# Around the Strassen up projection of a decoder layer: transposes moved behind two quads, difference blocks made in the stage before, the down projection's first inputs loaded in the last quads

## Chip, cores and metric

The kernel runs on one core of one Trainium2 chip. The metric is the device time in microseconds (us). TensorE multiplies (PE in the profile, PEld its weight loads), VectorE is DVE, ScalarE is ACT, GpSimd is POOL, SyncE is SP. SP's queue issues the loads from HBM, ACT's queue the stores.

## What is computed

One step of a decoder layer for 1024 prompt tokens and 8 x 4 sample tokens, model width 1024, all in float32:

```python
h = RMSNorm(x); z = h @ w_in            # u, v: chunked gMLP gating; q, k, v: windowed attention
...
merged = jnp.concatenate([rms_norm(a_out, g_out_chunk), rms_norm(b_out, g_out_attn)], axis=-1)
o = jnp.einsum('bsc,cd->bsd', merged, w_o)
x = x + rms_norm(o, g_post_mix)
h = rms_norm(x, g_pre_ffn)
f = jnp.einsum('bsf,fd->bsd', jnp.square(jax.nn.relu(jnp.einsum('bsd,df->bsf', h, w_up))), w_down)
return x + rms_norm(f, g_post_ffn)
```

The change touches the stretch from w_o to the first products with w_down; w_up is 1024 x 4096, w_down 4096 x 1024.

## The kernel before

Every product is made of three fp32r products: each operand is split into a rounded part (hi) and the rest (lo), by `split`, a cast on ACT (L127) and a subtraction on DVE (L128); the terms are hi x hi, hi x lo, lo x hi. The code is in program order on every engine queue where the text below speaks of it.

**The w_o stage.** The tokens are nine tiles: the 32 sample tokens (called NCH, first) and eight tiles of 128. `proj_o` multiplies a tile by w_o in two PSUM banks; the transposes of the next tile's merged inputs (`merge_transpose`, tiles mg, two buffers) and of the previous tile's hn stand inside this stream of matmuls. `post` (L832) then makes, tile by tile: the squares of both banks (ACT, L837), ms (DVE) and r (POOL, L137 and L143), x2 = o * r * g + x (L843, L844), its squares (L851), and hn (L854), which is the input of the up projection. x2 is stored to HBM. `h_store` (L857) transposes hn with eight transposes (L67) and splits it into hT hi and lo, in two column groups: group 0 with tiles 0 to 3 and the sample tokens, group 1 with tiles 4 to 7. The four sub-blocks of Strassen's method are the two halves of the input width (k 0 to 3 and 4 to 7) by the two halves of a group's columns.

`h_sums` (L813) makes the three difference blocks sg (hi and lo) that Strassen's products 6, 7 and 3 need, and replaces one block of hT by a sum. It first adds hi and lo again on POOL (L822), and it is called for tiles 2 and 3 and the sample tokens within the stage (group 0), and for group 1 after the first part of the first quad.

**The up projection.** A quad is one pair of weight blocks (16 pairs) by one column group (2): 7 products of 12 matmuls, in `first` (products 1 and 2), `second` (6, 5, 7) and `third` (4, 3). The banks A, C, B are PSUM; product 6 and those after it add into bank A, so a copy `s` of it (L938, ACT, `snap`) has to be made between them. The parts of neighbouring quads alternate: first of quad i, third of quad i-1, second of quad i. `up_weights` loads two 512 KB blocks of w_up per pair (SP) and forms seven weight units from them (subtractions L802, L803, L806, L808 on DVE, and a split of each); the first pair's blocks are loaded into the pool `stage` (tiles raw, three buffers) before the last tile's `post`, later ones into `rawp` (tiles rw, four buffers). The results are squared (`emit`) and stored to HBM as f_d.

The order in the first quads is (0,0), (1,0), (0,1), (1,1), that is pair and group. The last tile's `h_store` and pair 1's weights come after the first part of quad (0,0).

**The down projection.** In eight rounds of four f tiles, f_d is loaded back (`f_tile`, L1004) and split, w_down likewise (`pair`, L779), and `down_one` multiplies them. All of the first round's inputs are loaded after the last quad.

## Time and profile before

| | us |
|---|---|
| time, median of 3 runs | 1129.66 (1129.57 to 1130.35) |
| the profiled execution's own time | 1130.52 |
| its span | 1128.8, mean granted TensorE clock 0.982 |
| PE busy | 1073.3 (95%) |
| DVE busy | 687.9 (61%) |
| ACT busy | 429.7 (38%) |
| POOL busy | 77.6 (7%) |
| w_o stage, up projection, down projection (start of the first matmul) | 248, 373.9, 738.3 |

PE is the bound of the kernel in the long run, and its busy share says little of the single stages. Rows of the timeline give the start, the duration of the whole group of like instructions, the engine, the line, the operation, the tiles, the count, and in brackets the idle time of the engine before it with what ended it.

### The profile page before, as it was taken

To read this page: it belongs to the slowest core of one execution; us is meant where nothing else is said; L and a number is where in the kernel's file an instruction comes from. 1 tells how busy PE (TensorE), PEld (TensorE's weight loads), DVE (VectorE), ACT (ScalarE), POOL (GpSimd) and SP (SyncE) were. 2 spreads that over 40 slices of the span, in tenths; PEclk is the share of its full clock that TensorE was granted. 3 is DMA by queue.
4 is the path that set the end of the run, shared out by engine and by line. 5 is a ranking of instruction groups with operands and counts; after the bars stand their busy time and mean duration, and the time that the engine had idled before them with its cause. 6 is when DMAs were issued, how large, how long until landed. Compare 5 with 4: busy or idle time off the path is not lost.

```text
span 1128.8 us, 17897 instructions
## 1 busy us (share of the span) xinstructions
PE 1073.3 (95%) x7053; PEld 1004.8 (89%) x7053; DVE 687.9 (61%) x1335; ACT 429.7 (38%) x934; POOL 77.6 (7%) x97
## 2 busy tenths in 40 slices
PE   7999999999989689999999999689999999999996
PEld 5888777887867689999999999689999999999996
DVE  5777877776666877656655563364544635446256
ACT  6587966564443433333323322241221312203012
POOL 2100003110142300000000000000000000000001
PEclk9999999999999889999999999989999999999998
DMA  8332201235423324233323312372431514316025
GB/s 275 136 104 75 94 24 50 94 127 179 132 93 112 112 96 125 88 111 115 102 88 115 114 50 68 104 220 59 140 98 55 152 30 122 117 36 226 9 65 187
DMA packets 52228, 121.35 MB, mean 108 GB/s; under 512 B 6945, under 2 KB 16641, under 8 KB 52129
## 3 DMA queue, kind: packets, MB, share of 16 engines
q1 hardware_dynamic: 33312, 89.44, 25.8%
q10 hardware_dynamic: 18832, 30.78, 7.3%
q8 instruction: 55, 0.90, 0.3%
q14 instruction: 29, 0.23, 0.1%
HBM read 89.43 MB, written 31.82 MB: 107 GB/s over the span
## 4 chain that ended last, share of the span: by engine, by line
PE 82%; DVE 8%; ACT 4%; POOL 2%; issue 2%; DMA 2%; SPq 0%; DVEq 0%; ACTq 0%; POOLq 0%
PE z L64 70%; PE t L64 10%; PE t L67 3%; ACT sc L527 2%; DVE w L128 1%; POOL raw L822 1%; ACT w L130 1%; DVE hT_lo L128 1%; DVE w L1048 1%; DVE pT L128 0%; POOL ro L143 0%; DVE w L1061 0%; DMA raw<-in_w_v_dram 0%; DVE w L131 0%; DMA raw<-in_w_qkv_dram 0%
## 5 line engine op out<-in xcount | busy, mean ns | idle before, releaser
L64 PE MATMUL z<-f,w 128*128 128x400 f32 (+1 forms) x2304 | 374.2, 324 | 13.5 <-ACT w L127 13.5
L64 PEld LDWEIGHTS z<-f,w 128*128 128x128 f32 x2304 | 371.8, 189 | 14.3 <-ACT w L127 13.7
L64 PE MATMUL z<-w,hT_hi 128*128 128x512 f32 (+1 forms) x768 | 210.8, 381 | 0.4 <-DVE raw L191 0.4
L1019 DVE TENSOR_TENSOR acc<-z,acc 128x400 f32<-128x400 f32 (+1 forms) x168 | 86.5, 521 | 129.8 <-PE z L64 129.6
L64 PEld LDWEIGHTS z<-w,hT_hi 128*128 128x128 f32 x768 | 134.3, 189 | 25.2 <-DVE raw L191 0.8
L64 PE MATMUL z<-hT_hi,w 128*128 128x272 f32 (+1 forms) x768 | 146.8, 286 | 0.5 <-ACT s L938 0.5
L64 PE MATMUL z<-w,hT_lo 128*128 128x512 f32 (+1 forms) x384 | 124.5, 378 | 0.0
L64 PEld LDWEIGHTS z<-hT_hi,w 128*128 128x128 f32 x768 | 122.0, 189 | 0.7 <-ACT s L938 0.7
L127 ACT CAST f<-raw 128x544 fp32r<-128x544 f32 x64 | 38.7, 633 | 202.2 <-PE z L64 152.8
L64 PE MATMUL z<-hT_lo,w 128*128 128x272 f32 (+1 forms) x384 | 109.3, 285 | 0.0
L64 PE MATMUL z<-sg,w 128*128 128x272 f32 (+1 forms) x768 | 107.5, 290 | 0.0
L64 PEld LDWEIGHTS z<-sg,w 128*128 128x128 f32 x768 | 101.2, 195 | 0.0
L938 ACT COPY s<-z 128x272 f32<-128x272 f32 (+1 forms) x96 | 36.4, 380 | 144.3 <-PE z L64 141.6
L64 PEld LDWEIGHTS z<-w,hT_lo 128*128 128x128 f32 x384 | 67.6, 188 | 14.0
L64 PEld LDWEIGHTS z<-hT_lo,w 128*128 128x128 f32 x384 | 72.9, 190 | 0.0
L128 DVE TENSOR_TENSOR w<-w 128x512 fp32r<-128x512 f32 x64 | 44.6, 703 | 34.1 <-ACT w L127 32.8
L143 POOL TENSOR_TENSOR ro<-ms,neghalf 128x1 f32<-128x1 f32 (+1 forms) x18 | 11.9, 661 | 744.5 <-DVE ms L142 744.4
L128 DVE TENSOR_TENSOR f<-raw,f 128x544 fp32r<-128x544 f32 x64 | 44.0, 706 | 27.9 <-ACT f L127 27.8
L128 DVE TENSOR_TENSOR w<-raw,w 128x512 fp32r<-128x512 f32 x69 | 45.8, 703 | 20.6 <-ACT w L127 20.4
L64 PE MATMUL t<-sg,w 128*128 128x272 f32 (+1 forms) x384 | 54.1, 291 | 3.9 <-DVE fo L956 3.9
L64 PEld LDWEIGHTS t<-sg,w 128*128 128x128 f32 x384 | 50.7, 194 | 4.1 <-DVE fo L956 4.1
L967 DVE SCALAR_TENSOR_TENSOR fo<-fo 128x544 f32<-128x544 f32 (+1 forms) x64 | 45.3, 708 | 13.2 <-ACT fo L960 10.5
(208 smaller groups left out, 1337.2 us busy)
## 6 DMA issues: line engine op xcount, KB each, us to landing
raw<-in_w_down_dram SPq DMA_DIRECT2D x32, 512.0 KB, 4.3
rw<-in_w_up_dram SPq DMA_DIRECT2D x30, 512.0 KB, 3.7
f_d<-fo ACTq DMA_DIRECT2D x32, 272.0 KB, 3.1
raw<-f_d SPq DMA_DIRECT2D x32, 272.0 KB, 2.7
f_d<-fo ACTq DMA_DIRECT2D x32, 256.0 KB, 2.6
raw<-f_d SPq DMA_DIRECT2D x32, 256.0 KB, 2.7
xT<-in_xT_prompt_dram SPq DMA_DIRECT2D x8, 512.0 KB, 5.7
raw<-in_x_prompt_dram SPq DMA_DIRECT2D x8, 512.0 KB, 4.7
```

The source lines that it names most:

```text
L64: tc.keep_in_program_order(pe.matmul(out, lhsT, rhs, start=start, stop=stop, skip_group_check=resumed))
L67: tc.keep_in_program_order(pe.transpose(out, in_, ident[:n, :n]))
L127: pin(act.copy(hi, src))
L128: pin(vec.tensor_tensor(lo, src, hi.bitcast(F32), ALU.subtract))
L130: act.activation(hi, src, AF.Copy, scale=scale)
L143: pool.tensor_tensor(out, ms[:r, 0:1], neghalf[:r, 0:1], ALU.pow)
L527: act.activation(scs[kv][:, j, 0:nk], scs[kv][:, j, 0:nk], AF.Exp, scale=-1.0, bias=nm[:, h:h + 1], accum_out=lsum[:, h:h + 1])
L822: pool.tensor_tensor(r, hi[:, ks[k], c].bitcast(F32), lo[:, ks[k], c].bitcast(F32), ALU.add)
L938: act.copy(s, self.A)
L967: vec.scalar_tensor_tensor(f, f, 0.0, f, ALU.max, ALU.mult)
L1019: vec.tensor_tensor(o, ps[:, :n], o, ALU.add)
L1048: vec.tensor_tensor(self.y[:r, hs], tp[:r], g_fin[:r, hs], ALU.mult)
```

## The change

1. **w_o stage.** `h_sums` goes; `diffs` makes the same blocks straight from the transposes in PSUM, for tiles 2, 3 and the sample tokens, and for tile 6 inside the stage too. The block of the first half of columns (tiles t - 2) is added up again by `whole`, on DVE. There is one hn buffer (pool `hnp`) instead of two, x2 is kept in the tile xr, junk has one buffer, mg one instead of two (the sample's mg is a tile raw).
2. **First quads.** The weights of pairs 0 and 1 are both loaded into raw buffers, before the quads. The last tile's `h_store` comes ahead of quad 2, which is (0,1), instead of inside quad 0. `rawp` has two buffers instead of four. The memory for the copies s (pool `snap`), for f and for rw is that of the tiles hn and xr of the stage before.
3. **Last quads.** Their order is (14,0), (15,0), (14,1), (15,1) instead of pair by pair. In the second last one, behind group 0's last product, the memory of hT0 and sg0 is given to f tiles, and the first four f tiles and the first pair of w_down blocks are loaded and split. The other w_down blocks of round 0 come after the last quad.

```diff
-        mgp = pcm.enter_context(tc.tile_pool(name="mgp", bufs=2))
+        mgp = pcm.enter_context(tc.tile_pool(name="mgp", bufs=1))
...
-        mg = merge_load(NCH, mgp, "mg")
+        mg = merge_load(NCH, stage, "raw")
...
     pph = ExitStack()
     with ExitStack() as pcx:
         sg = [None, None]
+        sgp1 = pph.enter_context(tc.tile_pool(name="sgp1", bufs=1))
         psg0 = ExitStack()
         sgp0 = psg0.enter_context(tc.tile_pool(name="sgp0", bufs=1, side="right"))
-        sg[0] = [sgp0.tile([P, 3, 4, SUB[0]], F32R, name="sg0_%d" % i) for i in range(2)]
+        sg = [[p.tile([P, 3, 4, n], F32R, name="sg%d_%d" % (g, i)) for i in range(2)]
+              for g, (p, n) in enumerate(zip((sgp0, sgp1), SUB))]
+        hnp = pcx.enter_context(tc.tile_pool(name="hnp", bufs=1))
         mp = pcx.enter_context(tc.tile_pool(name="mp", bufs=2))
+        jp = pcx.enter_context(tc.tile_pool(name="jp", bufs=1))
         gcp = pcx.enter_context(tc.tile_pool(name="gcp", bufs=1))
         g_post = gcp.tile([P, D], F32, name="g_post")
...
-        def h_sums(g, x, n):
+        def diffs(g, x, n, r11, r12, r21, a22, s1, s2):
             hi, lo = hT[g]
             sh, sl = sg[g]
             ca, cb = slice(x, x + n), slice(SUB[g] + x, SUB[g] + x + n)
...
+            vec.tensor_tensor(s1, a22, r21, ALU.add)
+            vec.tensor_tensor(s2, s1, r11, ALU.subtract)
             split(sh[:, 0, :, ca], sl[:, 0, :, ca], s2)
-            split(hi[:, 0:4, cb], lo[:, 0:4, cb], r22)
-            vec.tensor_tensor(r21, r11, r21, ALU.subtract)
-            split(sh[:, 1, :, ca], sl[:, 1, :, ca], r21)
+            split(hi[:, 0:4, cb], lo[:, 0:4, cb], s1)
+            vec.tensor_tensor(r11, r11, r21, ALU.subtract)
+            split(sh[:, 1, :, ca], sl[:, 1, :, ca], r11)
             vec.tensor_tensor(r12, r12, s2, ALU.subtract)
             split(sh[:, 2, :, ca], sl[:, 2, :, ca], r12)
+        def h_transpose(hn, h, n):
+            tp = tbank()
+            for k in range(4):
+                transpose(tp[:, k * n:(k + 1) * n], hn[:n, (4 * h + k) * P:(4 * h + k + 1) * P], n)
+            return tp[:, 0:4 * n].rearrange("p (k c) -> p k c", k=4)
+        def halves():
+            t = stage.tile([P, D], F32, name="raw")
+            return [t[:, i * 512:(i + 1) * 512].rearrange("p (k c) -> p k c", k=4) for i in range(2)]
+        def whole(t):
+            hi, lo = hcols(t)
+            rs = halves()
+            for h, r in enumerate(rs):
+                vec.tensor_tensor(r, hi[:, 4 * h:4 * h + 4].bitcast(F32), lo[:, 4 * h:4 * h + 4].bitcast(F32), ALU.add)
+            return rs
+        def h_store(t, hn, firsts=None):
+            if t == NCH:
+                hi, lo = hT[0]
+                ca, cb = slice(2 * P, 2 * P + NSH), slice(SUB[0] + 2 * P, SUB[0] + 2 * P + NSH)
+                rs = [hnp.tile([P, 4, NSH], F32, name="rs", bufs=5) for _ in range(5)]
+                for h in range(2):
+                    tp = h_transpose(hn, h, NS)
+                    split(hi[:, 4 * h:4 * h + 4, ca], lo[:, 4 * h:4 * h + 4, ca], tp[:, :, 0:NSH])
+                    act.copy(rs[h], tp[:, :, 0:NSH])
+                    if h == 0:
+                        act.copy(rs[2], tp[:, :, NSH:NS])
+                split(hi[:, 4:8, cb], lo[:, 4:8, cb], tp[:, :, NSH:NS])
+                diffs(0, 2 * P, NSH, rs[0], rs[1], rs[2], tp[:, :, NSH:NS], rs[3], rs[4])
+            elif t % 4 < 2:
+                transpose_split(*hcols(t), hn, P)
+            else:
+                hi, lo = hcols(t)
+                g, c = gcol(t)
+                r11, r12 = firsts or whole(t - 2)
+                r21, s1 = halves()
+                s2 = halves()[0]
+                act.copy(r21, h_transpose(hn, 0, P))
+                tp = h_transpose(hn, 1, P)
+                split(hi[:, 4:8], lo[:, 4:8], tp)
+                diffs(g, c.start - SUB[g], P, r11, r12, r21, tp, s1, s2)
         def post(t, zo, xr):
             r = rows(t)
             ssq2 = small.tile([P, 2], F32, name="ssqo")
             for h in range(2):
-                junk = mp.tile([P, 512], BF16, name="junk", bufs=2)
+                junk = jp.tile([P, 512], BF16, name="junk")
                 act.activation(junk[:r], zo[h][:r], AF.Square, scale=D ** -0.5, accum_out=ssq2[:r, h:h + 1])
             ro = small.tile([P, 1], F32, name="ro")
             rms_scale2(ro[:r], ssq2[:r])
-            x2 = mp.tile([P, D], F32, name="x2")
+            hn = hnp.tile([P, D], F32, name="hn")
             for h in range(2):
                 hs = slice(h * 512, (h + 1) * 512)
-                vec.scalar_tensor_tensor(x2[:r, hs], zo[h][:r], ro[:r], g_post[:r, hs], ALU.mult, ALU.mult)
-            vec.tensor_tensor(x2[:r], x2[:r], xr[:r], ALU.add)
-            store(x2_d[drow(t), :], x2[:r])
-            if t == order[-1]:
-                hn = unit().bitcast(F32).rearrange("p a b -> p (a b)")
-            else:
-                hn = mp.tile([P, D], F32, name="hn")
+                vec.scalar_tensor_tensor(hn[:r, hs], zo[h][:r], ro[:r], g_post[:r, hs], ALU.mult, ALU.mult)
+            vec.tensor_tensor(xr[:r], hn[:r], xr[:r], ALU.add)
+            store(x2_d[drow(t), :], xr[:r])
             sx = small.tile([P, 1], F32, name="sx")
-            act.activation(hn[:r], x2[:r], AF.Square, accum_out=sx[:r])
+            act.activation(hn[:r], xr[:r], AF.Square, accum_out=sx[:r])
             r2 = small.tile([P, 1], F32, name="r2")
             rms_scale(r2[:r], sx[:r], D, EPS)
-            vec.scalar_tensor_tensor(hn[:r], x2[:r], r2[:r], g_ffn[:r], ALU.mult, ALU.mult)
+            vec.scalar_tensor_tensor(hn[:r], xr[:r], r2[:r], g_ffn[:r], ALU.mult, ALU.mult)
             return hn
...
             if t == order[-1]:
                 wup0 = up_weights(0, [stage.tile([P, D], F32, name="raw") for _ in range(2)])
+                firsts = whole(order[-3])
             hns.append((t, post(t, [fold(t, z) for z in zo], xr)))
         hn = hns[0][1]
         flush()
-    pcm.close()
+    rawp = pph.enter_context(tc.tile_pool(name="rawp", bufs=2, reuse_waits="tile"))
     sp_ = pph.enter_context(tc.tile_pool(name="snap", bufs=4, reuse_waits="tile"))
     fop = pph.enter_context(tc.tile_pool(name="fop", bufs=4, reuse_waits="tile"))
-    sgp1 = pph.enter_context(tc.tile_pool(name="sgp1", bufs=1, reuse_waits="tile"))
-    rawp = pph.enter_context(tc.tile_pool(name="rawp", bufs=4, reuse_waits="tile"))
-    sg[1] = [sgp1.tile([P, 3, 4, SUB[1]], F32R, name="sg1_%d" % i) for i in range(2)]
     def up_raws():
         return [rawp.tile([P, D], F32, name="rw") for _ in range(2)]
     class Quad:
-        def __init__(self, p, g, ws):
-            self.p, self.g, self.ws = p, g, ws
-            self.n = SUB[g]
-            self.A, self.C, self.B = [b[:, 0:self.n] for b in (zbank(), zbank(), tbank())]
+        def __init__(self, p, g):
+            self.p, self.g, self.n = p, g, SUB[g]
...
-        def first(self):
+        def first(self, ws):
             n = self.n
+            self.ws = ws
+            self.A, self.C, self.B = [b[:, 0:n] for b in (zbank(), zbank(), tbank())]
             self.fa = fop.tile([P, 2, SUB[0]], F32, name="fo")[:, :, 0:n]
             self.fb = fop.tile([P, 2, SUB[0]], F32, name="fo")[:, :, 0:n]
             self.product(1, self.A, True, True)
...
+    pq = ExitStack()
+    f_pools = []
+    def f_tile(ft):
+        f = f_pools[0 if ft % 9 < 7 else 1].tile([P, 2, T], F32R, name="f")
+        for g in range(2):
+            c = slice(GBASE[g], GBASE[g] + GW[g])
+            raw = raw_load(f_d[ft][:, c], [P, GW[g]])
+            split(f[:, 0, c], f[:, 1, c], raw)
+        return f
+    ws_up = {0: wup0, 1: up_weights(1, [stage.tile([P, D], F32, name="raw") for _ in range(2)])}
+    last = NPAIR - 2
+    seq = [(0, 0), (1, 0), (0, 1), (1, 1)] + [(p, g) for p in range(2, last) for g in range(2)]
+    seq += [(last, 0), (last + 1, 0), (last, 1), (last + 1, 1)]
+    quads = [Quad(p, g) for p, g in seq]
+    for i, q in enumerate(quads):
+        if i == 2:
+            h_store(order[-1], hn, firsts)
+        q.first(ws_up[q.p])
+        if i:
+            prev = quads[i - 1]
             prev.third()
             flush()
             if prev.g == 1:
                 del ws_up[prev.p]
                 if prev.p + 2 < NPAIR:
                     ws_up[prev.p + 2] = up_weights(prev.p + 2, up_raws())
+            if i == len(quads) - 2:
+                psg0.close()
+                phg0.close()
+                f_pools.append(pq.enter_context(tc.tile_pool(name="fp", bufs=7, side="right", reuse_waits="tile")))
+                fs0 = [f_tile(ft) for ft in range(FB)]
+                ws0 = pair(a["w_down"][0, 0])
         q.second()
-        prev = q
-        if (p, g) == (NPAIR - 1, 1):
-            q.third()
-            flush()
+    q.third()
+    flush()
     pph.close()
-    psg0.close()
-    phg0.close()
+    pcm.close()
     with ExitStack() as pf:
-        fp = pf.enter_context(tc.tile_pool(name="fp", bufs=FB + 4, side="right", reuse_waits="tile"))
+        pf.enter_context(pq)
+        f_pools.append(pf.enter_context(tc.tile_pool(name="fp2", bufs=2, reuse_waits="tile")))
         accp = pf.enter_context(tc.tile_pool(name="accp", bufs=1, reuse_waits="tile"))
         rp = pf.enter_context(tc.tile_pool(name="rp", bufs=2, reuse_waits="tile"))
         acc = accp.tile([P, KT, T], F32, name="acc")
...
+        def round_weights(b, dps):
+            return [w for dp in dps for w in pair(a["w_down"][b, dp])]
+        fs, ws = fs0, ws0 + round_weights(0, range(1, KT // 2))
         for b in range(NFB):
             last = b + 1 == NFB
             if not last:
-                nxt = round_inputs(b + 1)
+                nxt = ([f_tile((b + 1) * FB + i) for i in range(FB)], round_weights(b + 1, range(KT // 2)))
...
```

On VectorE at the end of the w_o stage, before, from the last tile but one's ms on (w_4063 and w_4066 are the lower halves of the first two weight units of pair 0, raw_4059 and raw_4060 the loaded blocks):

```order
L142 SCALAR_TENSOR_TENSOR ms_3977<-ssqo_3971 128x1
L843 SCALAR_TENSOR_TENSOR x2_3980<-z_3892,ro_3976,g_post_3172 128x512
L843 SCALAR_TENSOR_TENSOR x2_3980<-z_3893,ro_3976,g_post_3172 128x512
L128 TENSOR_TENSOR w_4063<-raw_4059,w_4063 128x512
L844 TENSOR_TENSOR x2_3980<-x2_3980,xr_3890 128x1024
L128 TENSOR_TENSOR w_4066<-raw_4059,w_4066 128x512
L802 TENSOR_TENSOR w_4069<-raw_4060,raw_4059 128x512
L806 TENSOR_TENSOR w_4069<-raw_4060 128x512
L136 TENSOR_SCALAR ms_3988<-sx_3985 128x1
L803 TENSOR_TENSOR w_4070<-raw_4060,w_4069 128x512
L854 SCALAR_TENSOR_TENSOR hn_3984<-x2_3980,r2_3987,g_ffn_3173 128x1024
```

The same place after (tile 7's post begins with ms_4111; raw_4035, raw_4038 and raw_4039 are inputs of tile 6's diffs; raw_4071 is pair 0's first loaded block):

```order
L142 SCALAR_TENSOR_TENSOR ms_4111<-ssqo_4105 128x1
L825 TENSOR_TENSOR raw_4035<-raw_4035,raw_4038 128x512
L128 TENSOR_TENSOR hT1_lo_91<-raw_4038,hT1_hi_90 128x4x128
L128 TENSOR_TENSOR sg1_1_3170<-raw_4039,sg1_0_3169 128x4x128
L128 TENSOR_TENSOR sg1_1_3170<-raw_4035,sg1_0_3169 128x4x128
L827 TENSOR_TENSOR raw_4035<-raw_4035,raw_4039 128x512
L884 SCALAR_TENSOR_TENSOR hn_4114<-z_3990,ro_4110,g_post_3183 128x512
L884 SCALAR_TENSOR_TENSOR hn_4114<-z_3991,ro_4110,g_post_3183 128x512
L128 TENSOR_TENSOR sg1_1_3170<-raw_4035,sg1_0_3169 128x4x128
L885 TENSOR_TENSOR xr_3988<-hn_4114,xr_3988 128x1024
L128 TENSOR_TENSOR w_4075<-raw_4071,w_4075 128x512
L128 TENSOR_TENSOR w_4078<-raw_4071,w_4078 128x512
```

The weight units of pair 0 have moved from inside tile 6's post behind the first half of tile 7's, and the diffs of tile 6 stand in their place; hn of tile 7 is hn_4114.

On VectorE a little later, after (xr_3988 holds x2 of tile 7, raw_4102 is the sum of tile 5, w_4081 and w_4082 hold differences of weights, fo_4173 is the first output of the first quad):

```order
L844 TENSOR_TENSOR raw_4102<-hT1_hi_90,hT1_lo_91 128x512
L812 TENSOR_TENSOR w_4082<-raw_4071,w_4082 128x512
L128 TENSOR_TENSOR w_4085<-w_4082,w_4085 128x512
L128 TENSOR_TENSOR w_4088<-w_4081,w_4088 128x512
L128 TENSOR_TENSOR w_4092<-w_4081,w_4092 128x512
L128 TENSOR_TENSOR w_4096<-w_4082,w_4096 128x512
L128 TENSOR_TENSOR w_4099<-raw_4072,w_4099 128x512
L844 TENSOR_TENSOR raw_4102<-hT1_hi_90,hT1_lo_91 128x512
L136 TENSOR_SCALAR ms_4121<-sx_4118 128x1
L891 SCALAR_TENSOR_TENSOR hn_4114<-xr_3988,r2_4120,g_ffn_3184 128x1024
L966 TENSOR_TENSOR fo_4173<-z_4171,s_4187 128x272
```

The hn of tile 7 stands behind all weight units of pair 0.

On ScalarE at the first quad, before (s_4147 is the first copy of bank A):

```order
L127 CAST w_4084<-w_4070 128x512
L127 CAST w_4087<-raw_4060 128x512
L837 ACTIVATE junk_4091,ssqo_4090<-z_3994 128x512
L837 ACTIVATE junk_4093,ssqo_4090<-z_3995 128x512
L938 COPY s_4147<-z_4130 128x272
L127 CAST hT1_hi_90<-raw_4208 128x4x128
L851 ACTIVATE w_4103,sx_4104<-x2_4099 128x1024
L60 DMA x2_d_97<-x2_4099 128x1024
L127 CAST hT1_hi_90<-t_4162 128x4x128
```

and after (s_4187 is that copy; z_4170 the bank A of quad 0):

```order
L127 CAST w_4075<-raw_4071 128x512
L127 CAST w_4078<-raw_4071 128x512
L888 ACTIVATE hn_4114,sx_4118<-xr_3988 128x1024
L60 DMA x2_d_97<-xr_3988 128x1024
L127 CAST w_4085<-w_4082 128x512
L127 CAST w_4088<-w_4081 128x512
L127 CAST w_4092<-w_4081 128x512
L127 CAST w_4096<-w_4082 128x512
L127 CAST w_4099<-raw_4072 128x512
L954 COPY s_4187<-z_4170 128x272
L127 CAST w_4143<-raw_4139 128x512
```

The copy has moved behind the squares of tile 7 and seven casts of pair 0's weights, and pair 1's first cast (w_4143) stands behind the copy.

On ScalarE in the last two quads, after (f_7767, f_7776 and f_7785 are f tiles, w_7796 and w_7799 the first w_down units, z_7843 the bank A of the last quad; the row ahead of these is its first copy):

```order
L127 CAST f_7767<-raw_7772 128x512
L127 CAST f_7776<-raw_7777 128x544
L127 CAST f_7776<-raw_7781 128x512
L978 ACTIVATE fo_7694<-z_7691 128x256
L60 DMA f_d28_126<-fo_7694 128x2x256
L127 CAST f_7785<-raw_7786 128x544
L127 CAST f_7785<-raw_7790 128x512
L60 DMA f_d29_127<-fo_7695 128x2x256
L954 COPY s_7917<-z_7843 128x256
L127 CAST w_7796<-raw_7794 128x512
L127 CAST w_7799<-raw_7794 128x512
L954 COPY s_7943<-z_7843 128x256
```

Before, no cast stands between the last quad's copies; the first f cast stands behind the last store to f_d. Now the casts of f and of the first w_down pair stand between them.

## Rows read from the trace of the kernel before

**Rows 1.** Waits of TensorE: line, releaser, us in total, times, longest us.

```profile
PE z L64 <- ACT w L127: 13.5, 1, 13.5
```

**Rows 2.** Timeline of TensorE, w_o stage: start us, us, engine, line, operation.

```profile
282.27 0.68 PE L67 MATMUL t<-ident,hn 32*128 32x32 f32 x8
...
287.12 1.03 PE L67 MATMUL t<-ident,hn 128*128 128x128 f32 x8
...
330.90 1.94 PE L67 MATMUL t<-ident,hn 128*128 128x128 f32 x8 [5.12 <-DVE hn L854]
332.49 1.85 PE L64 MATMUL z<-w,hT_hi 128*128 128x512 f32 x4
...
347.01 1.06 PE L67 MATMUL t<-ident,hn 128*128 128x128 f32 x8 [1.79 <-DVE hn L854]
347.83 1.17 PE L64 MATMUL z<-w,hT_hi 128*128 128x512 f32 x4
```

**Rows 3.** Timeline of VectorE, tile 1, and of GpSimd, tile 3, w_o stage.

```profile
304.51 1.41 DVE L843 SCALAR_TENSOR_TENSOR x<-z,ro,g_post 128x512 f32<-128x512 f32 x2 [0.73 <-POOL ro L143]
...
309.27 1.28 DVE L854 SCALAR_TENSOR_TENSOR hn<-x,r,g_ffn 128x1024 f32<-128x1024 f32 x1 [0.73 <-POOL r L137]
...
325.32 3.61 POOL L822 TENSOR_TENSOR raw<-hT_hi,hT_lo 128x512 f32<-128x512 f32 x2 [2.34 <-DVE sg L128]
328.89 0.55 POOL L137 TENSOR_TENSOR r<-ms,neghalf 128x1 f32<-128x1 f32 x1
```

**Rows 4.** Timeline of TensorE, from w_o to the third quad.

```profile
373.46 0.63 PE L64 MATMUL z<-w,hT_lo 128*128 128x512 f32 x2
...
386.55 1.94 PE L67 MATMUL t<-ident,w 128*128 128x128 f32 x8 [9.45 <-DVE w L854]
...
388.14 3.07 PE L64 MATMUL z<-sg,w 128*128 128x272 f32 x12
...
403.01 3.09 PE L64 MATMUL t<-sg,w 128*128 128x272 f32 x12 [3.85 <-DVE fo L956]
...
411.86 0.28 PE L64 MATMUL z<-hT_hi,w 128*128 128x256 f32 x1
```

**Rows 5.** Timeline of ScalarE and VectorE, first quads.

```profile
374.98 0.59 ACT L837 ACTIVATE junk<-z 128x512 bf16<-128x512 f32 x1
...
376.03 0.20 ACT L837 ACTIVATION_READ_ACCUMULATOR junk<-z 128x1 f32 x1
...
398.92 2.48 DVE L128 TENSOR_TENSOR w<-w 128x512 fp32r<-128x512 f32 x4
```

**Rows 6.** Busy time by windows, then timeline of VectorE, steady quads.

```profile
core 0: us, PE busy (x) PEld busy (x) DVE busy (x) ACT busy (x) POOL busy (x), PEclk, DMA share, GB/s
460.00:700.00 240.00, 240.00 (x1956) 240.00 (x1956) 140.00 (x236) 77.68 (x168) 0.00 (x0) 1.00 0.31 97
...
464.84 0.69 DVE L802 TENSOR_TENSOR w<-rw 128x512 f32<-128x512 f32 x1 [0.57 <-PE z L64]
...
477.46 0.69 DVE L128 TENSOR_TENSOR w<-rw,w 128x512 fp32r<-128x512 f32 x1 [0.34 <-ACT w L127]
```

**Rows 7.** TensorE at the down projection, its windows; costliest group of f casts.

```profile
723.19 1.60 PE L64 MATMUL t<-sg,w 128*128 128x256 f32 x12
...
738.32 6.86 PE L64 MATMUL z<-f,w 128*128 128x400 f32 x23 [13.53 <-ACT w L127]
...
739.00:741.00 2.00, 2.00 (x8) 1.93 (x7) 1.18 (x2) 1.14 (x2) 0.00 (x0) 0.50 0.72 209
...
743.00:744.00 1.00, 1.00 (x6) 0.99 (x5) 1.00 (x2) 0.31 (x1) 0.00 (x0) 0.72 0.78 276
...
L127 ACT CAST f<-raw 128x544 fp32r<-128x544 f32 x64 | 38.7, 633 | 202.2 <-PE z L64 152.8
```

**Rows 8.** DMA issues: tiles, queue, count, KB each, median us to landing.

```profile
raw<-in_w_down_dram SPq DMA_DIRECT2D x32, 512.0 KB, 4.3
...
rw<-in_w_up_dram SPq DMA_DIRECT2D x30, 512.0 KB, 3.7
...
raw<-in_w_up_dram SPq DMA_DIRECT2D x2, 512.0 KB, 6.1
```

More of the change, by code (lines that the diff above doesn't have):

```diff
@@ L816, in h_sums @@
             ca, cb = slice(x, x + n), slice(SUB[g] + x, SUB[g] + x + n)
-            ks = (slice(0, 4), slice(4, 8))
-            ts = [stage.tile([P, D], F32, name="raw") for _ in range(3)]
-            ts = [t[:, i * 512:i * 512 + 4 * n].rearrange("p (k c) -> p k c", k=4) for t in ts for i in range(2)]
-            r11, r12, r21, r22, s2 = ts[:5]
-            for r, k, c in ((r11, 0, ca), (r21, 0, cb), (r22, 1, cb), (r12, 1, ca)):
-                pool.tensor_tensor(r, hi[:, ks[k], c].bitcast(F32), lo[:, ks[k], c].bitcast(F32), ALU.add)
@@ L823, in h_sums @@
-            vec.tensor_tensor(r22, r21, r22, ALU.add)
-            vec.tensor_tensor(s2, r22, r11, ALU.subtract)
+            vec.tensor_tensor(s1, a22, r21, ALU.add)
+            vec.tensor_tensor(s2, s1, r11, ALU.subtract)
             split(sh[:, 0, :, ca], sl[:, 0, :, ca], s2)
-            split(hi[:, 0:4, cb], lo[:, 0:4, cb], r22)
-            vec.tensor_tensor(r21, r11, r21, ALU.subtract)
-            split(sh[:, 1, :, ca], sl[:, 1, :, ca], r21)
+            split(hi[:, 0:4, cb], lo[:, 0:4, cb], s1)
@@ L969, in emit @@
             store(f_d[2 * self.p + i][:, c0:c0 + 2 * self.n].rearrange("p (s c) -> p s c", s=2), f)
-    ws_up = {0: wup0}
-    seq = [(0, 0), (1, 0), (0, 1), (1, 1)] + [(p, g) for p in range(2, NPAIR) for g in range(2)]
-    prev = None
-    for i, (p, g) in enumerate(seq):
-        q = Quad(p, g, ws_up[p])
-        q.first()
-        if i == 0:
-            h_store(order[-1], hn)
-            ws_up[1] = up_weights(1, up_raws())
-            for x, n in ((0, P), (P, P)):
-                h_sums(1, x, n)
-        if prev:
+    pq = ExitStack()
[18 more added lines that the diff above has]
+            prev = quads[i - 1]
             prev.third()
@@ L1002, in hymba_step @@
         acc = accp.tile([P, KT, T], F32, name="acc")
-        def f_tile(ft):
-            f = fp.tile([P, 2, T], F32R, name="f")
-            for g in range(2):
-                c = slice(GBASE[g], GBASE[g] + GW[g])
-                raw = raw_load(f_d[ft][:, c], [P, GW[g]])
-                split(f[:, 0, c], f[:, 1, c], raw)
-            return f
         def down_one(b, fs, w, d, c0, n):
@@ L1063, in end @@
                 flush()
-        def round_inputs(b):
-            fs = [f_tile(b * FB + i) for i in range(FB)]
-            ws = []
-            for dp in range(KT // 2):
-                ws += pair(a["w_down"][b, dp])
-            return fs, ws
-        fs, ws = round_inputs(0)
+        def round_weights(b, dps):
+            return [w for dp in dps for w in pair(a["w_down"][b, dp])]
+        fs, ws = fs0, ws0 + round_weights(0, range(1, KT // 2))
         for b in range(NFB):
```

16 lines of the change are left out of this document (removed).

## Prediction

> **What bounds the kernel now.** I read the waits of TensorE first, then its timeline at the two ends of the up projection, then what the named releasers were doing. TensorE is the bound: in a stretch of 240 us in the middle of the up projection it has no gap, at a granted clock of 1.00, and VectorE and ScalarE are idle for 100 us of it and more [rows 6]. So only TensorE's gaps and its slow stretches can be won. The longest gap stands after the last quad: 13.53 us until the first down matmul, and then two 2 us samples of which one still runs at clock 0.50 and one second at 0.72 [rows 1, 7]. The second longest is that of the last tile, whose transposes come 9.45 us late, and the second quad's difference blocks come 3.85 us late [rows 4]. Two smaller gaps stand in the w_o stage, 5.12 and 1.79 us before the transposes of two tiles [rows 2]. What 1.00 and 0.50 mean is the two levels of 2.4 and 1.2 GHz; twelve matmuls take 1.60 us at the upper [rows 7] and 3.07 at the lower [rows 4]. I count on the lower level after each idle stretch of 4 us or more, since each such stretch here is followed by one; after 1.79 us there is none [rows 2].
>
> **A. The w_o stage.** The POOL additions of h_sums go. Two of them held POOL for 3.61 us, and the small r of the next tile, which hn needs, ran only behind them, at 328.89 [rows 3]. That is the stall of 5.12; behind it eight transposes took 1.94 instead of 1.06 and four matmuls 1.85 instead of 1.17 [rows 2], so 0.88 + 0.68 = 1.56 us more at the low clock. The same mechanism on VectorE's side made the 1.79. Removed: 5.12 + 1.79 + 1.56 = 8.5 us. The additions reappear as diffs on VectorE and ScalarE copies, from the transposes in PSUM, at some 0.62 us an operation (four took 2.48) [rows 5].
> New waits: hn has one buffer, so the first write of tile 0's hn waits for the sample tile's transposes, which end at 282.27 + 0.68 = 282.95 [rows 2]. From that write to the end of hn takes 309.27 + 1.28 - 304.51 = 6.04 us [rows 3], and the sample's small difference operations lie ahead in VectorE's queue (some 0.7 us, my estimate): 289.7, where the transposes now stand at 287.12 [rows 2]. I take 2.65 us. Later tiles write hn after their predecessor's transposes anyway, but tiles 3 and 4 have the diffs of the tile before ahead of them in VectorE's order, one operation of about 0.6 each [rows 5]: 1.2 us. Bounds for the new waits: 0 (the diffs fit in the gaps) and 6.5 (2.65, and three operations for each of two tiles). I take 3.85. **A gains 4.6.** The single mg buffer and the reuse of xr cost nothing: their loads are issued a whole tile (12.9 us: from 287.12 to 330.90 less the 5.12 is three tiles [rows 2]) ahead; without that cover each would cost a load of 3.7 [rows 8].
>
> **B. From the last w_o matmul to the third quad.** Today this is 411.86 - (373.46 + 0.63) = 37.8 us [rows 4]. Removed: the gap of 9.45 behind the first half of quad 0, and the 3.85 at the second quad. Added: the loads of pair 0's weights now share the staging buffers with tile 6's diffs. The first waits for the lower half of hT1 that is made from raw_4038 (in the order of VectorE shown above). With T the last w_o matmul: the two squares take 376.03 + 0.20 - 374.98 = 1.25 us [rows 5], so ms stands at T + 1.4, one subtraction and that lower half end at T + 2.8, the load takes 3.7 [rows 8], and after a cast the first matmul of quad 0 stands at T + 7.3, where today it follows with no gap. Each later load is behind that on SP's queue. If the load takes the 6.1 us that pair 0's loads show today [rows 8], add 2.4. I take 3.7, since today's two ran beside other traffic and the thirty of the up projection did not.
> The Trainium skill (DMA: Bandwidth & Descriptors, Anatomy of one DMA) gives a fit of 2.0 us plus the bytes at 436 GB/s, 3.2 us for 512 KB, measured on another issuing path; by it B would be 0.5 us better, and the measured 3.7 decides.
> Products 1 and 2 at the low clock, some 3.0 each, end at T + 13.4. The next product adds into the same bank and so needs the copy s of the first, and s lies in memory that hn and x2 of tile 7 held: it waits for the last write of hn_4114. Ahead of that on VectorE stand twelve operations, eleven of them on pair 0's weights, that wait for the loads; the first, the lower half of w_4075, ends at T + 8.3. Eleven more at about 0.6 [rows 5] end at T + 15.0, then come one addition, ms, the r on POOL (0.73 idle) and 1.28 for hn [rows 3]: T + 17.8, with the copy T + 18.1. So TensorE has a second gap of 4.7 us and is slow again: products 6, 5 and 7 take 2.9 + 2.7 + 1.6, to T + 25.3. First half of quad 1, 3.0; third part of quad 0, 3.0; second part of quad 1, 4.5; the eight transposes 1.0: the third quad begins at T + 36.9. **B gains 0.9.** Its ends: 2.4 worse by the load; 2.9 better if the second gap brings no low clock. The difference blocks of tile 7 come in the second part of quad 2, a quad and more after their inputs, and are covered.
>
> **C. Into the down projection.** The first four f tiles and the first pair of w_down are loaded and cast during the last two quads. Removed: 13.53 idle, and the low clock behind it, half of the 0.68 + 2 + 2 us up to 743 and 0.28 of the second after [rows 7]: 2.6. A quad is 84 matmuls, 84 x 240 / 1956 = 10.31 us [rows 6]. From the start S of the second last quad: the sixth f cast stands in ScalarE's order behind the first copy of the last quad, at S + 10.3 + 1.5 + 0.4, and ends with its lower half at about S + 15.0 (three casts at 0.63 [rows 7], the last's VectorE part). Then its buffer is free, the w_down load takes 4.3 [rows 8], and both casts are done at about S + 20.5. Behind them ScalarE has the copy of product 7, whose matmuls end at S + 20.3. So this just fits, and I charge 0.3 for it. With a landing of 6.1 instead of 4.3 [rows 8] it would cost 1.8 more. **C gains 15.8.** In the steady quads nothing changes; two raw buffers for weights instead of four are covered, see the second rival.
>
> **Sum.** 4.6 + 0.9 + 15.8 = 21.3 us. The profiled execution took 1130.52, so 1109.2 on its scale; it lies 0.86 above the median of 1129.66, so I say **1108.4 us**.
>
> **Rivals.**
> 1. *The down inputs are not hidden.* The last quads store f while eight f loads and a w_down load run. If these take turns with the stores, the w_down cast comes after the last quad and most of C falls to a new gap of up to 13 us with its slow clock: 1108.4 + 15.8 = 1124; half of it, 1116. Against it: the thirty loads of 512 KB land in 3.7 us in the same quads beside the same stores [rows 8]. The Trainium skill (Trainium Kernel Development and Optimization, Key Constraints) says that DMAs of the SP and ACT queues run on the same 16 engines and interleave; by that rule this rival would come about, at 1116 to 1124. The mean DMA share of 0.31 in the steady quads [rows 6] leaves room for both. Chance of more than half: 0.08.
> 2. *The weight loads of the up projection become exposed (slower).* With two raw buffers instead of four, the second tile of a pair is free only when its last lower half is done (477.46 + 0.69 = 478.15), and the next pair's first subtraction on it comes one pair after 464.84, at 464.84 + 20.6 = 485.5 [rows 6]. That leaves 7.3 us for a load of 3.7. From a landing of 7.3 us on, each us more is a us of idle TensorE, for some twelve pairs. At 9.1 it eats the whole gain of 21.3 (12 x 1.8), beyond that the kernel is slower: 11 us landing gives 1108.4 + 12 x 3.7 = 1153. For it: the loads in order on one queue, behind which nothing can pass. Against: the longest landing of such a load is 6.1. Chance 0.05, of which 0.03 slower.
> 3. *The boundary goes through without its gaps.* If pair 0's weights arrive before T and the copy does not wait for hn, the third quad would begin at about T + 18.5 (two quads of 84 matmuls less the third part of quad 1, and the transposes): 37.8 - 18.5 = 19.3 gained instead of 0.9, 1090. Against: the waits that I read from the order. Chance 0.07.
>
> **How the numbers follow.** My forecast has 0.80. Its ends are the bounds above: 1108.4 less 2.9 (no second low clock) and less 3.85 (no new waits in A) gives 1102; plus 2.4 (load), 1.8 (w_down), 2.65 (waits in A at their upper end) and part of the first rival gives 1117. These do not fall together often, and the three rivals outside hold 0.20. Two runs of this kernel can be told apart from about 0.2%, 2.3 us. Faster by more than that: the forecast, the first and the third rival, 0.95; within: 0.02; slower: 0.03.
>
> **What the profile after would show.** The idle of 13.5 before the first down matmul is gone and the first down matmuls run at clock 1.00. In the w_o stage no POOL operation of line 822 stands any more, the 5.12 is gone and a wait of about 2.7 stands before tile 0's transposes. At the boundary the first matmul of quad 0 waits some 7 us for a weight cast, product 6 some 5 us for a copy that waits for hn, and both are followed by clock 0.50. The third quad begins 37 us after the last w_o matmul; the steady quads take 10.3 us. I am wrong if the boundary has only one gap or none, if ScalarE waits for a weight load in steady quads, or if the last quad's product 4 waits for ScalarE by several us.

## The result and the profile after

The changed kernel takes 1110.05 us (median of 4 runs, 1108.61 to 1110.60) against 1129.62 before (4 runs): a ratio of 0.9825, 95% interval 0.9808 to 0.9842, some 19.6 us less. The forecast was 1108.4, from 1102 to 1117. The profiled execution took 1108.61, the fastest of the four; against the profiled execution of before, 1130.52, that is 21.9 us less, and the sum in the prediction was 21.3 on that scale.

TensorE's waits after (line, releaser, us in total, times, longest):

```profile
PE z L64 <- ACT w L127: 6.9, 1, 6.9
PE z L64 <- ACT s L954: 6.9, 2, 5.7
PE t L67 <- DVE hn L891: 4.0, 3, 2.5
```

The 13.5 of before [rows 1] and the 9.45 [rows 4] are gone, and two new waits stand at the first quad, for a weight cast and for the copy s. The places, in TensorE's timeline after:

```profile
289.85 1.07 PE L67 MATMUL t<-ident,hn 128*128 128x128 f32 x8 [2.47 <-DVE hn L891]
...
329.48 1.06 PE L67 MATMUL t<-ident,hn 128*128 128x128 f32 x8 [0.91 <-DVE hn L891]
...
343.04 1.06 PE L67 MATMUL t<-ident,hn 128*128 128x128 f32 x8 [0.64 <-DVE hn L891]
...
369.32 0.61 PE L64 MATMUL z<-w,hT_lo 128*128 128x512 f32 x2
376.88 0.59 PE L64 MATMUL z<-hT_hi,w 128*128 128x272 f32 x1 [6.95 <-ACT w L127]
...
388.01 3.09 PE L64 MATMUL z<-sg,w 128*128 128x272 f32 x12 [5.68 <-ACT s L954]
...
392.44 1.69 PE L64 MATMUL z<-sg,w 128*128 128x272 f32 x12
...
405.33 0.37 PE L64 MATMUL z<-hT_hi,w 128*128 128x256 f32 x1
...
716.01 0.39 PE L64 MATMUL z<-hT_hi,w 128*128 128x256 f32 x1 [1.26 <-ACT s L954]
...
718.98 8.30 PE L64 MATMUL z<-f,w 128*128 128x400 f32 x49
```

Against [rows 2, 4, 7] these rows give the gain by stretch. The last w_o matmul ends at 369.93 instead of 374.09: 4.2 us. From there to the third quad it is 35.4 us instead of 37.8: 2.4. From the third quad to the first down matmul it is 313.65 instead of 326.46, 12.8 us, and the down projection takes 387.9 instead of 390.5 us, 2.6, since it now starts at the upper clock. Together this is the whole difference of the two executions, 21.9. The clock shows in the windows after (us, busy times, then PEclk, DMA share, GB/s; PEclk is the granted TensorE clock, 1.00 the upper level and 0.50 the lower):

```profile
377.00:380.00 3.00, 2.57 (x10) 2.25 (x11) 3.00 (x6) 1.50 (x3) 0.00 (x0) 0.50 0.73 289
...
388.00:390.00 2.00, 1.99 (x9) 1.99 (x10) 1.92 (x4) 0.99 (x2) 0.00 (x0) 0.50 0.00 0
390.00:391.00 1.00, 1.00 (x6) 1.00 (x6) 1.00 (x3) 0.00 (x0) 0.00 (x0) 0.50 0.00 0
391.00:392.00 1.00, 1.00 (x10) 1.00 (x10) 0.61 (x2) 0.39 (x1) 0.00 (x0) 1.00 0.00 0
719.00:721.00 2.00, 2.00 (x14) 2.00 (x13) 1.12 (x2) 0.20 (x1) 0.00 (x0) 1.00 0.62 222
```

The lower clock follows the two new gaps at the first quad, for three to four microseconds each, and no longer stands at the start of the down projection.

### The profile page after: what moved, and what is told of

It is laid out like the page before. It is cut to its first block, busy times and chain, and to the rows that moved or that the text cites. A ratio compares the mean times of both kernels' runs of the same rounds, so it can differ in the third digit from the quotient of the medians.

```text
span 1106.9 us, 17857 instructions
## 1 busy us (share of the span) xinstructions
PE 1067.1 (96%) x7053; PEld 998.8 (90%) x7053; DVE 681.2 (62%) x1338; ACT 428.4 (39%) x936; POOL 52.2 (5%) x77
## 4 chain that ended last, share of the span: by engine, by line
PE 85%; DVE 7%; ACT 3%; issue 1%; DMA 1%; POOL 1%; SPq 0%; DVEq 0%; ACTq 0%; POOLq 0%
PE z L64 72%; PE t L64 10%; PE t L67 3%; ACT sc L527 1%; DVE hT_lo L128 1%; DVE w L1072 1%; DMA xT<-in_xT_prompt_dram 1%; DVE sg L128 1%; DVE pT L128 0%; DVE w L1085 0%; DMA raw<-in_w_down_dram 0%; DVE xr L885 0%; DVE w L131 0%; DVE hn L891 0%; ACT w L130 0%
## 5 line engine op out<-in xcount | busy, mean ns | idle before, releaser
L127 ACT CAST w<-raw 128x512 fp32r<-128x512 f32 x72 | 41.1, 618 | 39.9 <-DMA raw<-in_w_down_dram 34.0
L128 DVE TENSOR_TENSOR f<-raw,f 128x544 fp32r<-128x544 f32 x64 | 43.9, 705 | 18.0 <-ACT f L127 17.8
L64 PE MATMUL t<-hT_hi,w 128*128 128x272 f32 (+1 forms) x256 | 52.2, 285 | 0.0
```

The source lines that it names most:

```text
L64: tc.keep_in_program_order(pe.matmul(out, lhsT, rhs, start=start, stop=stop, skip_group_check=resumed))
L127: pin(act.copy(hi, src))
L128: pin(vec.tensor_tensor(lo, src, hi.bitcast(F32), ALU.subtract))
```

## The experiments

The experiments were run in groups, each on one chip and beside runs of the kernel before on that chip. The ratios are to those runs, so experiments of different groups are best compared by their ratios.

**Experiment 1: the same kernel again.**

> The changed kernel itself once more, as the measure for the others of this group. Theory (three gains: w_o stage 4.2, boundary 2.4, down start 15.4 us in the profiled execution): 1108.6 to 1110.6 us, the gaps at the same places: 2.5 before the sample-delayed transposes, 7.0 before the first quad, 5.7 before product 6, 1.3 in the last quad. Rival (part of the gain was the luck of one execution): some of these gaps differ by over 1 us, and the time with them.

1110.50 us (1108.99 to 1111.03), ratio 0.9824 (0.981 to 0.9837). The gaps named are the same within 0.2 us but for the last quad, 1.80 instead of 1.26. What differs is the clock behind the 2.5 us gap, in the timeline of this run:

```profile
289.87 1.07 PE L67 MATMUL t<-ident,hn 128*128 128x128 f32 x8 [2.48 <-DVE hn L891]
290.69 1.96 PE L64 MATMUL z<-w,hT_hi 128*128 128x512 f32 x4
...
331.04 1.06 PE L67 MATMUL t<-ident,hn 128*128 128x128 f32 x8 [0.92 <-DVE hn L891]
```

In the profiled execution of the changed kernel four such matmuls (the row at 290.69) took 1.19 at this place; here the clock fell, and tile 3's transposes come 1.56 us later (331.04 against 329.48). So one and the same gap is followed by the lower clock in one execution and not in another, and the profiled execution was one of the better.

**Experiment 4: the inputs of the down projection loaded after the last quad.**

```diff
-                fs0 = [f_tile(ft) for ft in range(FB)]
-                ws0 = pair(a["w_down"][0, 0])
...
+        fs0 = [f_tile(ft) for ft in range(FB)]
+        ws0 = pair(a["w_down"][0, 0])
         fs, ws = fs0, ws0 + round_weights(0, range(1, KT // 2))
```

> The first four f tiles and the first pair of w_down blocks are loaded after the last quad again; the order of the last quads and all else stay. Theory (all of the gain at the end is the early loading): a gap of about 13.5 us before the first down matmul with about 2.6 us of lower clock behind it, the 1.26 us wait in the last quad goes; 14 to 16 us slower than the changed kernel, about 1124.5. Rival (the new order of the last quads gives part of it, since the last f tiles stored are not those loaded first): a gap of 10 us or less, and less than 12 us slower.

1125.77 us, ratio 0.9961 (0.9948 to 0.9975): 15.3 slower than the changed kernel in the same group. Its first down matmul:

```profile
734.46 10.75 PE L64 MATMUL z<-f,w 128*128 128x400 f32 x51 [13.57 <-ACT w L127]
```

The gap is back in full, so the early loading and not the new order of the last quads is the gain; without it the wait in the last quad is 0.46, as in the kernel before, instead of 1.1 to 2.1 in the runs that load early in this order.

**Experiment 2: the copy s no longer lies over tile 7's x2.** The five tiles rs had pushed xr by 1280 bytes, so that the weight buffers ended inside it.

```diff
-                rs = [hnp.tile([P, 4, NSH], F32, name="rs", bufs=5) for _ in range(5)]
+                rs = [jp.tile([P, 4, NSH], F32, name="rs", bufs=5) for _ in range(5)]
```

> The five small tiles rs move from the pool of hn to that of junk, nothing else; so the two weight buffers cover hn and x2 of tile 7 exactly, and the copy s no longer lies over x2. The order of every engine stays. Theory (product 6 waits for the copy, and the copy for the last reading of x2): the gap before product 6 shrinks from 5.7 to about 1.5, since the copy then waits only for the casts ahead of it on ScalarE (they end at 383.2 against 387.6); product 6 runs at the upper clock; gain 4 to 6 us, less about 1 for pair 1's weights, so 1104 to 1106. Rival (the weight units of product 6 or the full queue of VectorE set that time): the gap stays above 4 us and the time within 1 us of the changed kernel.

1105.73 us (1105.18 to 1106.00), ratio 0.9783 (0.977 to 0.9797): 4.8 less than the changed kernel beside it. The order of the instructions is the same on every engine; the copy's wait for hn went. Product 6 in this run:

```profile
383.97 1.78 PE L64 MATMUL z<-sg,w 128*128 128x272 f32 x12 [1.56 <-ACT s L954]
```

A gap of 1.56 instead of 5.68, and the twelve matmuls at the upper clock. From the last w_o matmul to the third quad it is 31.3 us instead of 35.4 (35.7 in experiment 1), so the gain lies at this place. The wait of the copy for hn was the cause. A new wait of 0.82 for another copy stands in the second quad.

**Experiments 3 and 7: tile 7's transposes back behind the first part of quad 0**, in the changed kernel and in experiment 2.

```diff
-        if i == 2:
-            h_store(order[-1], hn, firsts)
         q.first(ws_up[q.p])
+        if i == 0:
+            h_store(order[-1], hn, firsts)
```

> Tile 7's transposes and difference blocks go back behind the first part of quad 0, as before; the rest is the changed kernel. Theory (the copy waits for the same hn that the transposes wait for, so moving them hides nothing as long as the copy waits): TensorE stands until about 387.5 before the transposes instead of 388.0 before product 6, the eight transposes take 1.9 at the lower clock instead of 1.0; time 0 to 1.5 us above the changed kernel. Rival (the move is what took away the 9.45 us gap): 4 us or more slower than the changed kernel, with a second gap for the difference blocks.

> Experiment 2 with tile 7's transposes and difference blocks put back behind the first part of quad 0, as in experiment 3. Theory (the move behind two quads is worth something only when the copy no longer waits for hn): TensorE waits about 5 us for hn before the transposes, the gain of experiment 2 is lost, 3.5 to 6 us slower than it, near the changed kernel's 1110. Rival (the place of the transposes never matters): within 1 us of experiment 2.

In the changed kernel: 1109.77 us (1108.30 to 1110.09), no difference from 1110.50. On top of experiment 2: 1109.02 (ratio 0.9814), 3.3 more than it, just under what was expected (in another group; the intervals 0.9801 to 0.9828 and 0.977 to 0.9797 don't meet). Its transposes:

```profile
387.72 1.94 PE L67 MATMUL t<-ident,hn 128*128 128x128 f32 x8 [5.11 <-DVE hn L891]
```

So the move behind two quads was worth nothing in the change as made, since a copy waited for the same hn, and some 3 us once it no longer does.

**Experiments 5 and 10: the sample's hn in a tile raw**, on top of experiment 2, twice.

```diff
-            hn = hnp.tile([P, D], F32, name="hn")
+            hn = stage.tile([P, D], F32, name="raw") if t == NCH else hnp.tile([P, D], F32, name="hn")
```

> On top of the copy's memory (experiment 2): hn of the sample tile lies in a tile raw, so that tile 0's hn needn't wait for the sample's transposes. Theory (that wait costs its 2.5 us in every execution and, in those executions where the clock falls after it, 1.5 us more): the gap before tile 0's transposes goes, the clock stays at 1.00 in that stretch in every profile, 2.5 to 4 us less than experiment 2, 1102 to 1103.5, and the spread of its runs is narrower. Rival (VectorE's queue, with the sample's difference operations ahead, sets tile 0's hn, not the buffer): the gap stays at 1.5 us or more and the time within 1 us of experiment 2.

> Experiment 5 once more, beside experiment 6 on the same chip: 1101.2 to 1102.5, a gap of about 1.5 us in the last quad.

1102.11 us (ratio 0.9751, 0.9737 to 0.9764) and 1101.34 (0.9741, 0.9727 to 0.9754), 3.6 and 4.4 below experiment 2 (in other groups; neither interval meets its 0.977 to 0.9797). The waits for hn of the first run:

```profile
PE t L67 <- DVE hn L891: 1.6, 2, 0.9
```

The wait of 2.5 is gone and the clock is 1.00 in that stretch in both profiles. The profile of experiment 2 has 1.00 there too, and against it the w_o stage ends 2.8 and 3.1 us earlier. So the waiting itself is worth about 3 us; the rest of the 3.6 and 4.4 would be executions with the lower clock behind it, which the times alone do not show. The spread did not become narrower (1.3 us in each, against 0.8 in experiment 2); that part of the expectation missed.

**Experiments 6 and 11: the w_down pair ahead of the f tiles**, on top of that, twice.

```diff
-                fs0 = [f_tile(ft) for ft in range(FB)]
                 ws0 = pair(a["w_down"][0, 0])
+                fs0 = [f_tile(ft) for ft in range(FB)]
```

> Experiment 5, and in the second last quad the pair of w_down blocks is loaded and cast ahead of the four f tiles instead of behind them. Theory (the last quad's product 4 waits 1.1 to 1.8 us because the copy after product 7 stands behind the casts of w_down, which land last): the gap in the last quad shrinks to below 0.8; 0.5 to 1.3 us less than experiment 5. Rival (whatever is loaded last holds up the copy, and the last f load does as well): the gap stays above 1 us, no difference.

> Experiment 6 once more. Theory (its gain of about 1 us is the shorter gap in the last quad): 0.5 to 1.3 us below experiment 5 of this group, with the gap in the last quad at 0.8 or less and the other gaps unchanged within 1 us. Rival (chance of single executions): the two medians change places or the gap does.

1101.03 us (0.9744, 0.9731 to 0.9757) and 1100.79 (0.9737, 0.9724 to 0.975). The last quad's wait, in the two runs, is 0.71 and 0.48 instead of 1.48 and 1.42; experiments 10 and 11:

```profile
708.31 0.39 PE L64 MATMUL z<-hT_hi,w 128*128 128x256 f32 x1 [1.42 <-ACT s L954]
...
707.42 0.39 PE L64 MATMUL z<-hT_hi,w 128*128 128x256 f32 x1 [0.48 <-ACT s L954]
```

That 0.8 to 0.9 us of waiting went is shown; in the times, 1.1 and 0.6 us lower, the intervals overlap, and they do not settle it. One other gap did move by over 1 us: product 6 of quad 0 waits 1.35 and 0.26 us in experiments 5 and 10, 0.41 and 1.63 in 6 and 11. It comes 6.8 to 6.9 us after the quad's first matmul in all four, so this cost nothing. This is the fastest kernel of the study, 29 to 30 us below before.

**Experiment 8: pair 0's first block loaded early**, on top of experiment 2.

```diff
-            if t == order[-1]:
-                wup0 = up_weights(0, [stage.tile([P, D], F32, name="raw") for _ in range(2)])
-                firsts = whole(order[-3])
             hns.append((t, post(t, [fold(t, z) for z in zo], xr)))
+            if t == order[-1]:
+                wup0 = up_weights(0, [mgp.tile([P, D], F32, name="mg"), stage.tile([P, D], F32, name="raw")])
+                firsts = whole(order[-3])
```

> Experiment 2, and the first block of pair 0's weights is loaded into the buffer of mg, which is free during the last w_o tile, with the calls that form the weights placed behind the last post. Theory (the 7 us before the first quad are the load of 3.7 us behind tile 6's difference blocks): the first matmul follows the last w_o matmul without a gap; but product 6 needs the second block, which is still loaded behind tile 6's blocks, and the copy stands on ScalarE behind pair 0's casts, so most of the 7 us comes back as a gap before product 6: from 1 us faster to 2 us slower than experiment 2. Rival (the first products alone set the boundary): 5 us or more faster than experiment 2.

1113.36 us, ratio 0.9855 (0.9841 to 0.9868): 7.6 slower than experiment 2, a miss. The gap before the first quad is gone as expected, but its two successors cost more:

```profile
388.45 3.09 PE L64 MATMUL z<-sg,w 128*128 128x272 f32 x12 [13.67 <-ACT s L954]
...
396.61 2.85 PE L64 MATMUL z<-sg,w 128*128 128x272 f32 x12 [2.63 <-ACT s L954]
```

VectorE and ScalarE in this run:

```profile
382.21 1.29 DVE L891 SCALAR_TENSOR_TENSOR hn<-xr,r,g_ffn 128x1024 f32<-128x1024 f32 x1 [0.44 <-POOL r L137]
...
385.22 0.69 DVE L812 TENSOR_TENSOR w<-mg,w 128x512 f32<-128x512 f32 x1
...
385.94 0.62 ACT L127 CAST w<-w 128x512 fp32r<-128x512 f32 x1 [3.13 <-DVE w L812]
...
386.46 1.66 ACT L127 CAST w<-raw 128x512 fp32r<-128x512 f32 x3
388.02 0.38 ACT L954 COPY s<-z 128x272 f32<-128x272 f32 x1
```

The copy stands on ScalarE behind all casts of pair 0. One of them waits 3.13 us for a difference (L812) that VectorE makes only behind tile 7's hn, since the edit puts the last post ahead of the weights. Two of the three casts from raw after it are pair 1's first ones, ahead of the copy too. The next quad's copy stands behind pair 1's other casts, which wait for the load of that pair's second block. The expectation had pair 0's casts and the second block's load; it left out tile 7's hn on VectorE and pair 1's casts. How much the 7 us gap itself would give with the copy ahead of the casts was not tried.

**Experiments 9 and 12: what made the 5.12 us gap of before**, two edits of the kernel before: the additions for group 0 on VectorE, and the sample's h_sums called behind tile 0 instead of tile 2.

```diff
-                pool.tensor_tensor(r, hi[:, ks[k], c].bitcast(F32), lo[:, ks[k], c].bitcast(F32), ALU.add)
+                (vec if g == 0 else pool).tensor_tensor(r, hi[:, ks[k], c].bitcast(F32), lo[:, ks[k], c].bitcast(F32), ALU.add)
```

> The kernel before with one edit: the four additions of each call of h_sums for group 0 run on VectorE instead of GpSimd; the order elsewhere is the scheduler's. Theory (the 5.12 us before tile 3's transposes is r queued behind two POOL additions): that gap falls below 2.5 us and its low clock goes; the additions add about 0.6 us each to VectorE's queue, so a gap of 1 to 2.5 us may stand before one or two tiles; 4 to 6.5 us less than before, 1124 to 1126. Rival (any engine that does these sums delays hn as much): a gap of 4 us or more remains and the time is within 2 us of before.

```diff
+                if t == 0:
+                    h_sums(0, 2 * P, NSH)
                 if t in (2, 3):
                     h_sums(0, (t % 2) * P, P)
-                    if t == 2:
-                        h_sums(0, 2 * P, NSH)
```

> The kernel before with one edit: the sample tokens' h_sums is called behind tile 0's h_store instead of tile 2's; the additions stay on GpSimd. Theory now (experiment 9 has shown that POOL is not the only cause: the sample's sixteen small operations and tile 2's differences stand together in tile 3's post): without the sample's operations there, the second half of x2 comes about 2.4 us earlier and POOL's two big additions too, the gap of 5.12 us shrinks below 3 us; 2 to 4.5 us less than before, 1126 to 1128.5. Rival (the volume of tile 2's own differences and additions alone makes the gap): it stays at 4 us or more, and the time within 1 us of before.

The first takes 1130.92 us, ratio 1.0003 (0.9994 to 1.0012), no difference; the second 1129.08, ratio 0.9992 (0.9983 to 1.0001), 1.0 us less by the medians and at most some 2 by the interval. Tile 3's transposes in the one and in the other:

```profile
330.06 1.94 PE L67 MATMUL t<-ident,hn 128*128 128x128 f32 x8 [4.17 <-DVE hn L854]
```

```profile
329.51 1.94 PE L67 MATMUL t<-ident,hn 128*128 128x128 f32 x8 [3.77 <-DVE hn L854]
```

Without any big addition on POOL 4.17 of the 5.12 us stay. What they are shows on VectorE, where x2 is made in two halves and ms, which r needs, comes after it; first in experiment 9, then in the kernel before:

```profile
317.91 0.75 DVE L843 SCALAR_TENSOR_TENSOR x<-z,ro,g_post 128x512 f32<-128x512 f32 x1 [0.44 <-POOL ro L143]
...
323.51 0.74 DVE L843 SCALAR_TENSOR_TENSOR x<-z,ro,g_post 128x512 f32<-128x512 f32 x1
...
327.45 0.14 DVE L136 TENSOR_SCALAR ms<-sx 128x1 f32<-128x1 f32 x1
```

```profile
321.87 0.74 DVE L843 SCALAR_TENSOR_TENSOR x<-z,ro,g_post 128x512 f32<-128x512 f32 x1
...
324.30 0.74 DVE L843 SCALAR_TENSOR_TENSOR x<-z,ro,g_post 128x512 f32<-128x512 f32 x1
...
327.79 0.15 DVE L136 TENSOR_SCALAR ms<-sx 128x1 f32<-128x1 f32 x1
```

In experiment 9 the second half comes 5.6 us after the first, and in between VectorE works without a pause on the sums and differences of tile 2 and of the sample. In the kernel before, ms ends at 327.94 and POOL's additions at 328.93 [rows 3], so they held r up by about 1 us, which is what experiment 9 took off the gap. The rest stands on VectorE ahead of ms; in the kernel before VectorE also waits 2.09 us there for sums that POOL makes, and in experiment 9 it makes them itself, so the additions cost time on either engine. The time did not follow, since tile 4's wait grew from 1.79 to 2.19 and the lower clock came behind it. Without the sample's operations 3.77 stay, between what the two theories asked, and the time is the rival's; tile 2's differences still stand ahead of tile 3's x2 there, and wait for POOL. How the rest divides among tile 2's operations is not shown by an edit of its own.

## Why the prediction was right, point by point

**The w_o stage**: forecast 4.6, measured 4.2. The new waits were 2.47 + 0.91 + 0.64 = 4.0 against the 3.85 taken, at the tiles named. What was removed had the right size, since the 8.5 us stand in [rows 2], but the reason given for its largest part was wrong: experiment 9 takes the additions off POOL and 4.17 of the 5.12 remain. The step that failed is "That is the stall of 5.12", which read the last releaser as the cause; the additions ahead of r on POOL held it up by about 1 us, and the rest stands ahead of x2 and ms on VectorE. That the gap does shrink to 0.91 in the changed kernel comes with the change of this stage as a whole; which part of it does this was not separated, and neither was what made the 1.79.

**The boundary**: forecast 0.9, measured 2.4. The two waits and their times came as worked out: the first matmul 6.95 us after the last of w_o (7.3 said), the copy's start at 387.57, 17.6 us after it (17.8), product 6 at 18.1 (18.1). VectorE's rows after show the chain that was read from the order, its last step ending 0.16 us before ScalarE's copy:

```profile
386.13 1.28 DVE L891 SCALAR_TENSOR_TENSOR hn<-xr,r,g_ffn 128x1024 f32<-128x1024 f32 x1 [0.73 <-POOL r L137]
```

The mis-sized term is the second low clock: products 6, 5 and 7 were said to take 2.9 + 2.7 + 1.6 and took 2.9 + 1.5 + 1.5, since the upper clock was back during product 5. That is 1.2 of the 1.5 us. The last matmuls of quad 0's first part were at the upper clock too, from 380.9 on; this gave nothing, since product 6 waited for the copy. The load landed as taken, from the row of the thirty loads and not from the 6.1 of today's two:

```profile
raw<-in_w_up_dram SPq DMA_DIRECT2D x4, 512.0 KB, 3.8
```

**The down projection**: forecast 15.8, measured 12.8 + 2.6 = 15.4, and experiment 4 gives back 15.3. The 2.6 of low clock came as taken; both 2 us samples behind the gap of before are at 0.50, as the sum has it and the prediction's first paragraph does not:

```profile
741.00:743.00 2.00, 2.00 (x8) 1.97 (x7) 0.89 (x3) 0.83 (x2) 0.00 (x0) 0.50 0.79 270
```

The wait in the last quad was sized at 0.3 and is 1.26. The chain of waits after shows where (start, us, what):

```profile
709.54 4.99 DMA raw<-in_w_down_dram
...
714.55 1.14 ACT w L127 x2
715.68 0.28 ACT s L954
...
716.01 1.70 PE z L64 x12
```

The w_down load took 4.99 us instead of the 4.3 charged, 0.7 of the 1.0 that was missing; it was within the bound of 6.1. The Trainium skill (Trainium Kernel Development and Optimization, Key Constraints) says that DMAs of the SP and ACT queues run on the same 16 engines and interleave. The 4.99 agrees with it in direction, beside f loads and f stores, though no run shows that these made the load longer; the price was 1 us and not the rival's 8 to 16.

**The rivals.** The down inputs were hidden but for that wait. The weight loads of the steady quads are not exposed: from 440 to 680 TensorE is busy throughout.

```profile
440.00:680.00 240.00, 240.00 (x1957) 240.00 (x1956) 145.88 (x246) 81.56 (x175) 0.00 (x0) 1.00 0.33 103
```

The boundary without gaps did not come by itself; experiment 2 removes most of one gap of the two and gives 4.8 us.

**The median** lies 1.4 us above the profiled execution, where before it lay 0.86 below. The prediction carried that 0.86 over. The step behind it, that only an idle stretch of 4 us or more is followed by the lower clock, failed: the 2.5 us wait for the sample's buffer is so followed in some executions. The kernel before had a sign of it: behind its 3.85 us [rows 4] twelve matmuls took 3.09, the time of the lower clock. The three other runs of the changed kernel have a mean granted clock of 0.987 to 0.990 against 0.993 in the profiled one, which fits; they have no trace, so it is not shown that this wait made the difference.

**Luck.** That 1108.4 lies within 2 us of 1110.05 is in part chance. The boundary came out 1.5 us better than forecast, the two other stretches 0.8 worse together, and the step from the profiled execution to the median 2.3 worse.

## What to carry to other kernels

When a stage's memory is given to the next, look up which new tile lies over which old one: a small tile that shifts the layout by 1280 bytes put a copy behind a whole chain of VectorE work, and moving that tile, with the order of the instructions unchanged, gave back 4.8 us. A row that names the releaser of a wait names the last one; before an engine is blamed, look when the inputs of the waiting operation were ready, or take the engine's work away and see whether the gap stays. And work moved off the critical path gains nothing while another instruction at the old place waits for the same result.

## What was not expected of the hardware

The same gap of 2.5 us is followed by the lower clock in some executions and not in others: of the seven profiles with it (the changed kernel twice, experiments 2, 3, 4, 7 and 8), two show a mean granted clock of 0.84 from 289 to 300 us, experiment 4 and the changed kernel's second, and five 1.00. It costs some 1.5 us where it falls. In experiment 9 a gap of 2.19 us before tile 4's transposes was followed by it too; they took 1.71 us instead of 1.06:

```profile
346.70 1.71 PE L67 MATMUL t<-ident,hn 128*128 128x128 f32 x8 [2.19 <-DVE hn L854]
```

The wait of 2.05 us in the last quad of experiment 8 was not: the granted clock is 1.00 from 722 to 724 us.
